# RMSNorm with SiLU on one core: six blocks of four rows in flight become four slots of six rows, with loads and stores on other queues

## The chip, the core and the metric

The kernel runs on one core of a Trainium2 chip. The core has a TensorE (PE), a VectorE (DVE), a ScalarE (ACT), a GpSimd (POOL) and a SyncE (SP); data come from the chip's memory (HBM) into the on-chip memory of 128 partitions by DMA. In this profile the core's transfers run on 16 DMA engines, and a transfer is issued from the queue of SP or of ACT. The metric is the device time of one execution in microseconds (us). The time before is the median of three runs.

## The reference

```python
def setup_inputs():
    batch, seq_len, hidden = 8, 1024, 2048
    return {
        "x": np.random.randn(batch, seq_len, hidden).astype(np.float32),
        "gamma": np.random.randn(hidden).astype(np.float32),
        "eps": np.float32(1e-5),
    }

def reference(x: np.ndarray, gamma: np.ndarray, eps: np.float32) -> np.ndarray:
    rms = np.sqrt(np.mean(x ** 2, axis=-1, keepdims=True) + eps)
    out = gamma * x / rms
    return (out * (1 / (1 + np.exp(-out)))).astype(np.float32)
```

There are 8192 rows of 2048 floats. Each row is divided by its root mean square, multiplied by gamma, and put through SiLU. 67.1 MB are read and 67.1 MB written.

## The kernel before

The rows are cut into 16 blocks of 512. A block lies on 128 partitions with four rows (J = 4) on each, one after the other, so that a partition holds 32 KB that are contiguous in HBM too. Six blocks (BUFS = 6) can be on the chip at once. In this text a "row" of a block means row j of all partitions: 128 x 2048 floats, 1 MB.

Before the blocks, gamma comes in as one row by a DMA from SP (L110), four matmuls with a column of ones spread it over the partitions (L113), and DVE copies it out of PSUM to g (L115). ACT then copies one element of the same tile (L116), which holds it until the copy to g is done; after that it issues loads 2 to 5. Loads 0 and 1 are issued before.

The work on one block:

- load (L54): one DMA of 4 MB from ACT's queue.
- squares: the sum of squares of each row, of which ACT takes the first one or two (L65, Square with accumulation) and DVE the others (L73). share(b) says how many ACT takes.
- root and invert: ACT's Sqrt of the mean plus eps (L82), DVE's reciprocal (L87).
- multiply: DVE multiplies each row by its reciprocal root and by g, in place (L92).
- silu: ACT's Silu on two rows at a time, in place (L98), then the store.
- store (L102): one DMA of 4 MB from SP's queue.

ACT needs a table load when it goes from Square or Silu to Sqrt, and from Sqrt to Silu; these are rows of their own in the profile.

The order is written out by hand (the body under manual_schedule is issued in the order of the program, engine by engine). In the loop over b, the squares and the root of block b + 1 are issued beside the multiply and silu of block b: for the first three blocks, ACT's squares of b + 1 come before the silus of b and DVE's squares of b + 1 after the multiplies of b; in the middle, all squares and the root of b + 1 come before the multiplies and silus of b. The load of block b + 3 is issued from ACT after its first square of block b + 1, once six blocks are under way; it waits for the store of the block that had its buffer. The last block is done differently: DVE multiplies by g alone (L155), the reciprocal comes between, and ACT's Silu takes it as its scale, row by row (L157); one store follows.

Of the kernel before, what the change touches and what calls it, by code (L numbers as in the profile page):

```python
# [1 line left out]

# [4 lines left out]

ACT = mybir.ActivationFunctionType
ALU = mybir.AluOpType


@with_exitstack
def kernel(
    ctx: ExitStack,
    tc: tile.TileContext,
    x: bass.AP,
    gamma: bass.AP,
    eps: bass.AP,
    out: bass.AP,
):  # L20

    nc = tc.nc
    P = nc.NUM_PARTITIONS
    f32 = mybir.dt.float32
    x2 = x.flatten_outer_dims()
    o2 = out.flatten_outer_dims()  # L30
    n, d = x2.shape
    J = 4
    BUFS = 6
    nblk = n // (P * J)
    xb = x2.rearrange("(b p j) d -> b p (j d)", p=P, j=J)
    ob = o2.rearrange("(b p j) d -> b p (j d)", p=P, j=J)

    singles = ctx.enter_context(tc.tile_pool(name="singles", bufs=1))
    pool = ctx.enter_context(tc.tile_pool(name="pool", bufs=BUFS))
    small = ctx.enter_context(tc.tile_pool(name="small", bufs=2))  # L40
    psum = ctx.enter_context(tc.tile_pool(name="psum", bufs=1, space=bass.MemoryType.PSUM))

    Q = 4
    w = d // Q
    g = singles.tile([P, d], f32)
    eps_t = singles.tile([P, 1], f32)
    ones = singles.tile([P, P], f32)
    junk_a = psum.tile([P, d], f32, name="junk_a")
    junk_v = psum.tile([P, d], f32, name="junk_v")
    blocks, sss, rmss, rstds = {}, {}, {}, {}  # L50

    def load(b):
        xt = pool.tile([P, J * d], f32, name="xt")
        nc.scalar.dma_start(out=xt, in_=xb[b])  # L54
        blocks[b] = xt

    def row(b, j):
        return blocks[b][:, j * d:(j + 1) * d]

    def squares_scalar(b, loads=()):  # L60


        sss[b] = small.tile([P, J], f32, name="ss")
        for j in range(share(b)):
            nc.scalar.activation(out=junk_a, in_=row(b, j), func=ACT.Square,  # L65
                                 accum_out=sss[b][:, j:j + 1])
            if j == 0:
                for s in loads:
                    load(s)

    def squares_vector(b):
        for j in range(share(b), J):
            nc.vector.tensor_tensor_reduce(  # L73
                out=junk_v, in0=row(b, j), in1=row(b, j), scale=1.0, scalar=0.0,
                op0=ALU.mult, op1=ALU.add, accum_out=sss[b][:, j:j + 1])

    def share(b):
        return 1 if 4 <= b <= 12 and b % 2 == 0 else 2

    def root(b):  # L80
        rms = small.tile([P, J], f32, name="rms")
        nc.scalar.activation(out=rms, in_=sss.pop(b), func=ACT.Sqrt, scale=1.0 / d, bias=eps_t)  # L82
        rmss[b] = rms

    def invert(b):
        rstd = small.tile([P, J], f32, name="rstd")
        nc.vector.reciprocal(out=rstd, in_=rmss.pop(b))  # L87
        rstds[b] = rstd

    def multiply(b):  # L90
        for j in range(J):
            nc.vector.scalar_tensor_tensor(out=row(b, j), in0=row(b, j), scalar=rstds[b][:, j:j + 1],  # L92
                                           in1=g, op0=ALU.mult, op1=ALU.mult)

    def silu(b):
        for h in range(0, J, 2):
            cols = slice(h * d, (h + 2) * d)
            nc.scalar.activation(out=blocks[b][:, cols], in_=blocks[b][:, cols], func=ACT.Silu)  # L98
        store(b)

    def store(b):
        nc.sync.dma_start(out=ob[b], in_=blocks[b])  # L102

    with tc.manual_schedule():

        load(0)
        nc.vector.memset(ones, 1.0)  # L107
        nc.vector.memset(eps_t, float(eps))
        nc.scalar.activation(out=junk_a[:, 0:1], in_=ones[:, 0:1], func=ACT.Square)  # L109
        nc.sync.dma_start(out=g[0:1, :], in_=bass.AP(tensor=gamma.tensor, offset=gamma.offset, ap=[[d, 1], [1, d]]))  # L110
        for c in range(Q):
            cols = slice(c * w, (c + 1) * w)
            nc.tensor.matmul(junk_v[:, cols], ones[0:1, :], g[0:1, cols], start=True, stop=True)  # L113
        load(1)
        nc.vector.tensor_copy(out=g, in_=junk_v)  # L115
        nc.scalar.copy(out=junk_a[:, 0:1], in_=junk_v[:, d - 1:d])  # L116
        for b in range(2, BUFS):
            load(b)

        last = nblk - 1
        SOON = 3
        squares_scalar(0)
        squares_vector(0)
        root(0)
        invert(0)
        for b in range(last):
            loads = [b + 3] if BUFS <= b + 3 < nblk else []
            if b < SOON:  # L130
                multiply(b)
                squares_scalar(b + 1, loads)
                silu(b)
                squares_vector(b + 1)
                root(b + 1)
            elif b < last - 1:
                squares_scalar(b + 1, loads)
                squares_vector(b + 1)
                root(b + 1)
                multiply(b)  # L140
                silu(b)
            else:
                multiply(b)
                squares_scalar(b + 1)
                silu(b)
                squares_vector(b + 1)
                root(b + 1)
            if b + 1 < last:
                invert(b + 1)


        for j in range(J):
            if j == J // 2:
                invert(last)
            nc.vector.tensor_mul(out=row(last, j), in0=row(last, j), in1=g)  # L155
        for j in range(J):
            nc.scalar.activation(out=row(last, j), in_=row(last, j), func=ACT.Silu,  # L157
                                 scale=rstds[last][:, j:j + 1])
        store(last)


# [1 line left out]
_INS = ['x', 'gamma', 'eps']  # L163
_OUTS = [((8, 1024, 2048), 'float32')]

_NUMBERS = {'eps': 9.999999747378752e-06}


# [26 lines left out]
```

## Time and profile before

| what | value |
|---|---|
| median of 3 runs | 317.02 us (316.7 to 317.08) |
| span of the profiled execution | 315.1 us |
| DVE busy | 235.3 us (75%), 157 instructions |
| ACT busy | 213.9 us (68%), 137 instructions |
| PE busy | 7.2 us (2%) |
| HBM read, written | 67.12 MB, 67.11 MB: 426 GB/s over the span |
| load: issue to landing, median | 38.7 us for 4 MB |
| store: issue to landing, median | 29.0 us for 4 MB |

The span runs from the first to the last instruction of one profiled execution; the runs' time has some 1.9 us more around it. An engine is busy while it executes an instruction; instructions that issue DMAs or wait are not counted. In the row of slices each digit is a tenth of busy time in one fortieth of the span (7.9 us). A group's row gives the line, the engine, the operation, its output and inputs, the count, then busy us and mean ns of one, then the idle time of the engine just before and what ended it. The chain of waits follows the work that ended last, backwards from the end. A DMA packet here is what one DMA engine moves for one partition of a transfer: 32 KB in a block's load or store. Each packet has a record with its start and its duration in the trace.

### The profile page before, as it was taken

The page shows a single profiled execution, that of the slowest core. Times are in us where ns is not written, and L with a number is a line of the kernel's source. Part 1 is how long each engine was busy: PE and PEld are TensorE (multiplying, and loading weights), DVE is VectorE, ACT ScalarE, POOL GpSimd, SP SyncE. Part 2 cuts the span into 40 slices and gives each one's busy share as a digit, 9 for nine tenths or more (in the row PEclk, how much of TensorE's full clock was granted, in tenths as well). Part 3 has the DMA queues.
Part 4 walks back from the last instruction along what each step waited for, and adds up shares of the span by engine and source line. Part 5 has one row for each costly group of instructions (what it writes and reads, how often), then busy time and mean ns, then how long its engine had stood idle before and what let it go on. Part 6 is the DMA issues. An engine that isn't in the chain of part 4 may idle for free.

```text
span 315.1 us, 439 instructions
## 1 busy us (share of the span) xinstructions
PE 7.2 (2%) x8; PEld 2.5 (1%) x8; DVE 235.3 (75%) x157; ACT 213.9 (68%) x137; POOL 0.2 (0%) x4
## 2 busy tenths in 40 slices
PE   6200000000000000000000000000000000000000
PEld 2000000000000000000000000000000000000000
DVE  0679697979895695957969489593995939999600
ACT  1269998972799258682687827877278768779910
POOL 0000000000000000000000000000000000000000
DMA  8999999999999999999999999999999999999997
GB/s 334 412 453 416 383 458 408 462 403 462 403 459 408 454 412 458 408 462 403 462 403 462 408 458 408 458 408 458 416 449 416 449 416 449 428 437 428 437 428 308
DMA packets 4613, 134.24 MB, mean 426 GB/s; under 512 B 514, under 2 KB 514, under 8 KB 514
## 3 DMA queue, kind: packets, MB, share of 16 engines
q10 hardware_dynamic: 2304, 67.11, 49.8%
q1 hardware_dynamic: 2306, 67.12, 49.3%
q14 instruction: 3, 0.02, 0.0%
HBM read 67.12 MB, written 67.11 MB: 426 GB/s over the span
## 4 chain that ended last, share of the span: by engine, by line
DMA 68%; DVE 14%; ACT 11%; issue 1%; ACTq 1%; DVEq 0%
DMA xt<-in_x_dram 68%; DVE xt L92 9%; DVE junk_v L73 5%; ACT xt L98 4%; ACT junk_a L65 3%; ACT xt L157 2%; ACT L82 1%; ACTq L190 1%; ACT L157 0%; ACT L98 0%; ACT rms L82 0%; DVE ss L73 0%; ACTq L54 0%; DVE rstd L87 0%; ACT L109 0%
## 5 line engine op out<-in xcount | busy, mean ns | idle before, releaser
L92 DVE SCALAR_TENSOR_TENSOR xt<-xt,rstd,g 128x2048 f32<-128x2048 f32 x60 | 137.0, 2346 | 0.1
L98 ACT ACTIVATE xt<-xt 128x4096 f32<-128x4096 f32 x30 | 108.3, 3615 | 27.4 <-DVE xt L92 27.4
L73 DVE CUSTOM_DVE_ANT_0 junk_v<-xt 128x2048 f32<-128x2048 f32 x37 | 85.1, 2299 | 42.9 <-DMA xt<-in_x_dram 42.2
L65 ACT ACTIVATE junk_a<-xt 128x2048 f32<-128x2048 f32 x27 | 50.7, 1876 | 16.1 <-DMA xt<-in_x_dram 14.0
L82 ACT ACT_TABLE_LOAD x15 | 19.2, 1283 | 26.6 <-DVE ss L73 26.5
L98 ACT ACT_TABLE_LOAD x14 | 18.0, 1283 | 0.2
L115 DVE COPY g<-junk_v 128x2048 f32<-128x2048 f32 x1 | 2.3, 2292 | 9.0 <-PE junk_v L113 9.0
L87 DVE RECIPROCAL rstd<-rms 128x4 f32<-128x4 f32 x16 | 2.7, 172 | 8.4 <-ACT rms L82 8.4
L155 DVE TENSOR_TENSOR xt<-xt,g 128x2048 f32<-128x2048 f32 x4 | 8.9, 2277 | 0.0
L82 ACT ACTIVATE rms<-ss,eps_t 128x4 f32<-128x4 f32 x16 | 4.8, 297 | 5.7 <-DVE ss L73 5.5
L157 ACT ACTIVATE xt<-xt,rstd 128x2048 f32<-128x2048 f32 x4 | 7.7, 1991 | 0.0
L113 PE MATMUL junk_v<-g,ones 1*128 1x512 f32 x8 | 7.2, 1072 | 2.8 <-DMA g<-in_gamma_dram 2.8
L116 ACT COPY junk_a<-junk_v 128x1 f32<-128x1 f32 x1 | 0.1, 144 | 9.8 <-DVE g L115 9.8
L73 DVE DVE_READ_ACCUMULATOR2_ANT ss<- 128x1 f32 x37 | 5.2, 141 | 0.0
L65 ACT ACTIVATION_READ_ACCUMULATOR junk_a<-xt 128x1 f32 x27 | 5.0, 186 | 0.0
L113 PEld LDWEIGHTS junk_v<-g,ones 1*128 1x128 f32 x8 | 2.5, 325 | 5.9 <-issue 5.9
L109 ACT ACT_TABLE_LOAD x1 | 1.3, 1283 | 1.1 <-PEq L176 1.1
L157 ACT ACT_TABLE_LOAD x1 | 1.3, 1283 | 0.0
L107 DVE MEMSET ones<- 128x128 f32 x1 | 0.2, 165 | 0.8 <-PEq L176 0.8
L109 ACT ACTIVATE junk_a<-ones 128x1 f32<-128x1 f32 x1 | 0.2, 174 | 0.0
L176 POOL MEMSET const-bfloat16-1.0<- 128x1 bf16 x1 | 0.1, 103 | 0.0
L176 POOL MEMSET const-uint8-127<- 128x1 uint8 x1 | 0.1, 102 | 0.0
(3 smaller groups left out, 0.3 us busy)
## 6 DMA issues: line engine op xcount, KB each, us to landing
xt<-in_x_dram ACTq DMA_DIRECT2D x16, 4096.0 KB, 38.7
out_dram<-xt SPq DMA_DIRECT2D x16, 4096.0 KB, 29.0
g<-in_gamma_dram SPq DMA_DIRECT2D x1, 8.0 KB
```

Source lines behind the costliest of these rows:

```text
L65: nc.scalar.activation(out=junk_a, in_=row(b, j), func=ACT.Square, accum_out=sss[b][:, j:j + 1])
L73: nc.vector.tensor_tensor_reduce(out=junk_v, in0=row(b, j), in1=row(b, j), scale=1.0, scalar=0.0, op0=ALU.mult, op1=ALU.add, accum_out=sss ...
L82: nc.scalar.activation(out=rms, in_=sss.pop(b), func=ACT.Sqrt, scale=1.0 / d, bias=eps_t)
L87: nc.vector.reciprocal(out=rstd, in_=rmss.pop(b))
L92: nc.vector.scalar_tensor_tensor(out=row(b, j), in0=row(b, j), scalar=rstds[b][:, j:j + 1], in1=g, op0=ALU.mult, op1=ALU.mult)
L98: nc.scalar.activation(out=blocks[b][:, cols], in_=blocks[b][:, cols], func=ACT.Silu)
L109: nc.scalar.activation(out=junk_a[:, 0:1], in_=ones[:, 0:1], func=ACT.Square)
L113: nc.tensor.matmul(junk_v[:, cols], ones[0:1, :], g[0:1, cols], start=True, stop=True)
L115: nc.vector.tensor_copy(out=g, in_=junk_v)
L155: nc.vector.tensor_mul(out=row(last, j), in0=row(last, j), in1=g)
L157: nc.scalar.activation(out=row(last, j), in_=row(last, j), func=ACT.Silu, scale=rstds[last][:, j:j + 1])
L190: with _tile.TileContext(nc) as tc:
```

## The change

The blocks have different sizes now: one of two rows, one of four, nine of six, and one of four, 64 rows of a partition as before. They live in four slots of six rows (48 KB of a partition); the first slot takes the blocks of two and four rows together at first. A block's DMA moves 16, 32 or 48 KB per partition, contiguous on both sides. Loads are issued from SP in the order of the blocks; the load into a slot that was used waits for all its stores. Stores are issued from ACT after the block's last Silu; the last block's store is two DMAs of two rows each. Gamma's load moves to ACT, and the copy of one element (L116 before) is gone.

compute(b) issues a whole block before the next one begins: half of the squares on DVE, half on ACT, Sqrt, reciprocal, multiplies, Silus, store. For blocks 0, 1, 2 and 11 (SCALED) DVE multiplies by g alone and the Silu takes the reciprocal root as its scale, row by row; the first of these multiplies is issued before the reciprocal. The others multiply by both on DVE and have Silus of two rows.

```diff
+FILLINGS = [
+    [(2, 2), (4, 4)],
+    [(6, 6)],
...
+    [(6, 6)],
+    [(4, 2)],
+]
+SLOTS = 4
+
+SCALED = (0, 1, 2, 11)
...
-    J = 4
-    BUFS = 6
...
-    pool = ctx.enter_context(tc.tile_pool(name="pool", bufs=BUFS))
-    small = ctx.enter_context(tc.tile_pool(name="small", bufs=2))
+    pool = ctx.enter_context(tc.tile_pool(name="pool", bufs=SLOTS))
+    small = ctx.enter_context(tc.tile_pool(name="small", bufs=3))
...
+    def load(b, slot):
+        b.slot = slot
+        nc.sync.dma_start(out=rows(b, 0, b.rows), in_=b.x)
...
+    def fill(k):
+        slot = pool.tile([P, ROWS * d], f32, name="xt")
+        for b in fillings[k]:
+            load(b, slot)
...
+    def compute(b):
+        J = b.rows
+        half = J // 2
...
+        for j in range(half):
             nc.vector.tensor_tensor_reduce(
+                out=junk_v, in0=rows(b, j), in1=rows(b, j), scale=1.0, scalar=0.0,
+                op0=ALU.mult, op1=ALU.add, accum_out=ss[:, j:j + 1])
+        for j in range(half, J):
+            nc.scalar.activation(out=junk_a, in_=rows(b, j), func=ACT.Square,
+                                 accum_out=ss[:, j:j + 1])
+        nc.scalar.activation(out=rms[:, 0:J], in_=ss[:, 0:J], func=ACT.Sqrt, scale=1.0 / d, bias=eps_t)
+        scaled = b.number in SCALED
         for j in range(J):
+            if j == (1 if scaled else 0):
+                nc.vector.reciprocal(out=rstd[:, 0:J], in_=rms[:, 0:J])
+            if scaled:
+                nc.vector.tensor_mul(out=rows(b, j), in0=rows(b, j), in1=g)
+            else:
+                nc.vector.scalar_tensor_tensor(out=rows(b, j), in0=rows(b, j), scalar=rstd[:, j:j + 1],
+                                               in1=g, op0=ALU.mult, op1=ALU.mult)
+        step = 1 if scaled else 2
+        for j in range(0, J, step):
+            if scaled:
+                nc.scalar.activation(out=rows(b, j), in_=rows(b, j), func=ACT.Silu,
+                                     scale=rstd[:, j:j + 1])
+            else:
+                nc.scalar.activation(out=rows(b, j, 2), in_=rows(b, j, 2), func=ACT.Silu)
+            k = b.per_store
+            if (j + step) % k == 0:
+                first = j + step - k
+                nc.scalar.dma_start(out=b.out[:, first * d:(first + k) * d], in_=rows(b, first, k))
 
     with tc.manual_schedule():
-
-        load(0)
+        slot = pool.tile([P, ROWS * d], f32, name="xt")
+        load(fillings[0][0], slot)
         nc.vector.memset(ones, 1.0)
         nc.vector.memset(eps_t, float(eps))
+        nc.scalar.dma_start(out=g[0:1, :], in_=bass.AP(tensor=gamma.tensor, offset=gamma.offset, ap=[[d, 1], [1, d]]))
         nc.scalar.activation(out=junk_a[:, 0:1], in_=ones[:, 0:1], func=ACT.Square)
-        nc.sync.dma_start(out=g[0:1, :], in_=bass.AP(tensor=gamma.tensor, offset=gamma.offset, ap=[[d, 1], [1, d]]))
...
-        load(1)
+        for b in fillings[0][1:]:
+            load(b, slot)
         nc.vector.tensor_copy(out=g, in_=junk_v)
-        nc.scalar.copy(out=junk_a[:, 0:1], in_=junk_v[:, d - 1:d])
-        for b in range(2, BUFS):
-            load(b)
...
+        for k in range(1, SLOTS):
+            fill(k)
+        for k in range(len(fillings)):
+            for b in fillings[k]:
+                compute(b)
+            if k + SLOTS < len(fillings):
+                fill(k + SLOTS)
```

More of the change, by code (lines that the diff above doesn't have):

```diff
@@ L9 @@
 ALU = mybir.AluOpType
+FILLINGS = [
+    [(2, 2), (4, 4)],
+    [(6, 6)],
+    [(6, 6)],
+    [(6, 6)],
+    [(6, 6)],
+    [(6, 6)],
+    [(6, 6)],
+    [(6, 6)],
+    [(6, 6)],
+    [(6, 6)],
+    [(4, 2)],
+]
+SLOTS = 4
+SCALED = (0, 1, 2, 11)
 @with_exitstack
@@ L31 @@
     n, d = x2.shape
-    J = 4
-    BUFS = 6
-    nblk = n // (P * J)
-    xb = x2.rearrange("(b p j) d -> b p (j d)", p=P, j=J)
-    ob = o2.rearrange("(b p j) d -> b p (j d)", p=P, j=J)
+    ROWS = max(sum(j for j, _ in f) for f in FILLINGS)
+    assert sum(j for f in FILLINGS for j, _ in f) * P == n
     singles = ctx.enter_context(tc.tile_pool(name="singles", bufs=1))
-    pool = ctx.enter_context(tc.tile_pool(name="pool", bufs=BUFS))
-    small = ctx.enter_context(tc.tile_pool(name="small", bufs=2))
+    pool = ctx.enter_context(tc.tile_pool(name="pool", bufs=SLOTS))
+    small = ctx.enter_context(tc.tile_pool(name="small", bufs=3))
     psum = ctx.enter_context(tc.tile_pool(name="psum", bufs=1, space=bass.MemoryType.PSUM))
@@ L49 @@
     junk_v = psum.tile([P, d], f32, name="junk_v")
[L50 to L90, printed above, removed]
-        for j in range(J):
[L92 to L99, printed above, removed]
@@ L101, in store @@
-    def store(b):
-        nc.sync.dma_start(out=ob[b], in_=blocks[b])
+    class Block:
+        pass
+    fillings, at, number = [], 0, 0
+    for f in FILLINGS:
+        blocks, r = [], 0
+        for j, per_store in f:
+            b = Block()
+            b.rows, b.per_store, b.offset, b.number = j, per_store, r, number
+            number += 1
+            b.x = x2[at:at + j * P, :].rearrange("(p j) d -> p (j d)", p=P, j=j)
+            b.out = o2[at:at + j * P, :].rearrange("(p j) d -> p (j d)", p=P, j=j)
+            blocks.append(b)
+            r += j
+            at += j * P
+        fillings.append(blocks)
@@ new lines, in load, with rows @@
+    def load(b, slot):
[5 more added lines that the diff above has]
+            load(b, slot)
+    def rows(b, j, k=1):
+        return b.slot[:, (b.offset + j) * d:(b.offset + j + k) * d]
+    def compute(b):
+        J = b.rows
+        half = J // 2
+        ss = small.tile([P, ROWS], f32, name="ss")
+        rms = small.tile([P, ROWS], f32, name="rms")
+        rstd = small.tile([P, ROWS], f32, name="rstd")
+        for j in range(half):
+            nc.vector.tensor_tensor_reduce(
+                out=junk_v, in0=rows(b, j), in1=rows(b, j), scale=1.0, scalar=0.0,
[5 more added lines that the diff above has]
+        scaled = b.number in SCALED
+        for j in range(J):
+            if j == (1 if scaled else 0):
[16 more added lines that the diff above has]
+                nc.scalar.dma_start(out=b.out[:, first * d:(first + k) * d], in_=rows(b, first, k))
@@ L113 @@
             nc.tensor.matmul(junk_v[:, cols], ones[0:1, :], g[0:1, cols], start=True, stop=True)
-        load(1)
+        for b in fillings[0][1:]:
+            load(b, slot)
         nc.vector.tensor_copy(out=g, in_=junk_v)
-        nc.scalar.copy(out=junk_a[:, 0:1], in_=junk_v[:, d - 1:d])
-        for b in range(2, BUFS):
-            load(b)
[L122 to L159, printed above, removed]
+        for k in range(1, SLOTS):
[5 more added lines that the diff above has]
+                fill(k + SLOTS)
 _INS = ['x', 'gamma', 'eps']
```

## The prediction

> **What bounds the kernel now.** I read the slices of the span first, then the stretches, then the chain, then the costliest groups. Slices and queues:
>
> ```profile
> DVE  0679697979895695957969489593995939999600
> ACT  1269998972799258682687827877278768779910
> DMA  8999999999999999999999999999999999999997
> DMA packets 4613, 134.24 MB, mean 426 GB/s; under 512 B 514, under 2 KB 514, under 8 KB 514
> q10 hardware_dynamic: 2304, 67.11, 49.8%
> q1 hardware_dynamic: 2306, 67.12, 49.3%
> ```
>
> The DMA row is 9 from the second slice to the last but one, while DVE and ACT have holes everywhere. q10 (loads) and q1 (stores) together took 99.1% of the 16 engines' time. The stretches (stretch, its length, five engines, clock, DMA share, GB/s):
>
> ```profile
> 24.00:34.00 10.00, 0.00 (x0) 0.00 (x0) 9.95 (x7) 9.94 (x7) 0.00 (x0) 1.00 1.01 436
> 34.00:42.00 8.00, 0.00 (x0) 0.00 (x0) 5.17 (x4) 7.91 (x8) 0.00 (x0) 1.00 0.97 373
> 42.00:66.00 24.00, 0.00 (x0) 0.00 (x0) 22.19 (x14) 21.23 (x11) 0.00 (x0) 1.00 1.01 437
> 66.00:279.00 213.00, 0.00 (x0) 0.00 (x0) 169.33 (x115) 144.74 (x90) 0.00 (x0) 1.00 1.00 433
> 279.00:300.00 21.00, 0.00 (x0) 0.00 (x0) 17.46 (x11) 20.68 (x13) 0.00 (x0) 1.00 1.00 434
> ```
>
> 433 GB/s is the pace with loads and stores mixed (66 to 279) and with stores nearly alone (from 279). Only 24 to 66 is below it: (10 x 436 + 8 x 373 + 24 x 437) / 42 = 424.6, so 42 x 8.4 / 433 = 0.8 us is lost where the first store comes in. The chain says the same, long stretches of loads end to end, and then the last block's work, under stores that still run:
>
> ```profile
> 104.80 38.98 DMA xt<-in_x_dram
> 143.78 0.02 issue
> 143.80 0.01 ACT junk_a L65
> 143.81 38.65 DMA xt<-in_x_dram
> ...
> 297.10 1.89 ACTq L190
> 298.99 1.89 ACT xt L157
> ```
>
> So the bytes bound it. 134.2 MB at 433 is 310.0 us. The span of 315.1 has 5.1 us more: about 2.1 until the first packet starts, 0.6 in the first packets (1.8 us each in the packet records instead of 1.21), 0.8 at the first store, 0.85 from the last packet to the end, and 0.8 that I don't resolve. The median of the runs, 317.02, is 1.9 above the span; I carry that over unchanged.
>
> **The change part by part.** "Row" is 8 KB on each of 128 partitions, 1.049 MB, or 2.42 us at 433 GB/s.
>
> *Longer runs.* A DMA gives each engine 8 packets, one per partition. Before: 32 block DMAs, 256 packets of 32 KB per engine. After: 12 loads and 13 stores, 200 packets of 16, 32 or 48 KB. Bytes are the same. What a packet costs beside its bytes comes from two records of different size in the packet records: 8 KB fetches in mid-run take 0.309 us, and the 32 KB packets 1.210 apiece by their count in 66 to 279 (175.9 per engine in 213 us). That makes 0.300 per 8 KB and 0.0085 fixed. Saved: 56 x 0.0085 = 0.48, and 7 semaphore packets of 0.009, 0.06. I take -0.5 us. Bounds: -0.1 if 48 KB packets pay in proportion to their bytes; -0.6 with 0.009, the whole time of a 4-byte packet, as the fixed part. The 48 KB size itself is in no row.
>
> [...]
>
> *Queues.* Loads go to SP, where 0.33 us (row of the gamma issue) replaces 0.38 (ACT's issue of block 0); both began at 0.73, so the first packet moves by under 0.1 us: nothing. L116, which held loads 2 to 5 back to 12.38, is gone; loads 0 and 1 covered that until 22.7, so nothing is gained. Thirteen stores cost ACT 13 x 0.4 = 5 us. Behind each on ACT wait the next block's squares; they wait for a load anyhow.
>
> *The first store.* It can start once g is there: copy of g ends at 12.3, DVE square 2.44, table load and sqrt 1.6, table load 1.28, two silus 3.9: issued near 21.5 instead of 35.18. Before, its first packet started 4.8 us after the issue, and two load packets per engine ran 0.4 us long each. I keep 0.8; bounds 0.4 (only half recurs) and 1.2 (it grows with 48 KB packets): -0.4 to +0.4.
>
> *Serial blocks.* No block's squares are now issued ahead of the block before's silus. These are the rows of the chain:
>
> ```profile
> L92 DVE SCALAR_TENSOR_TENSOR xt<-xt,rstd,g 128x2048 f32<-128x2048 f32 x60 | 137.0, 2346 | 0.1
> L98 ACT ACTIVATE xt<-xt 128x4096 f32<-128x4096 f32 x30 | 108.3, 3615 | 27.4 <-DVE xt L92 27.4
> L73 DVE CUSTOM_DVE_ANT_0 junk_v<-xt 128x2048 f32<-128x2048 f32 x37 | 85.1, 2299 | 42.9 <-DMA xt<-in_x_dram 42.2
> L82 ACT ACT_TABLE_LOAD x15 | 19.2, 1283 | 26.6 <-DVE ss L73 26.5
> ```
>
> From a landing to the store's issue, for six rows: three DVE squares 3 x (2.30 + 0.14) = 7.3 (ACT's three, 6.1, beside them), table load and sqrt 1.6, reciprocal 0.2, six multiplies at the pitch of 2.285 (four in 9.14) 13.7, the last pair's silu 3.6: 26.4 us. A block's bytes in and out need 12 x 2.42 = 29.1. So compute keeps up by 2.7 us a block. I cost it at nothing; the cover is the store queue. Followed from the start: store 0's first packet at about 27.5 (21.5, 4.8, and 1.2 for longer load packets), done by 47 (8 turns of a 16 KB store and a 48 KB load packet, 2.43 each); store 1 is ready at 37.6, done by 71 (8 turns of 3.03); store 2 is ready near 60, store 3 near 85, due at 100, then one in 29.1. Each is ready over 9 us before its turn. If the cover went, every us per block beyond it would be DMA idle time.
>
> *Four slots.* A refill on SP waits for all stores of its slot; only later loads queue behind it. Slot 0 is free at 71, and the loads already issued last to about 82: 11 us of cover, the same in later rounds. If it went, stores alone would keep the 433.
>
> *The tail.* Here it is closest. In the packet records of before, loads and stores take turns, one packet each apart from occasional pairs, and a packet takes 1.21 whether or not the other queue runs. So a load DMA pairs with a store DMA, whatever their sizes. By 27.5, (27.5 - 2.1 - 0.6 - 0.8) / 2.42 = 9.9 rows are loaded: blocks 0, 1 and 0.65 of block 2. The remaining 9.35 load DMAs pair with 9.35 stores, so when the last load ends, block 9 has 0.65 x 6 = 3.9 rows to store: 9.4 us. Block 10 landed 8 x (1.21 + 1.82) = 24.2 us earlier, and its first store packet is ready 26.4 + 0.4 issue + 1.3 (issue to first packet, from block 0) = 28.1 after landing, 3.9 after the last load. Slack 5.5 us. Block 11 follows on ACT: squares 4.1, table and sqrt 1.6, table 1.3, two silus 3.9, so its first half is ready some 12.6 us after block 10, whose store takes 14.5. The halves therefore hide behind it and gain nothing: the bytes already last to the end. I take 0.
>
> [...]
>
> Sum: 317.02 - 0.5 = 316.5, with bounds of -1.0 to +0.3 around 317.02.
>
> **The rivals.**
> 1. *Turns go by bytes, and the tail runs dry.* Then small stores don't lag, the store queue empties in the first blocks, and later each store starts when it is ready, 28.1 after its landing, 1.0 before block 10's landing. The last load needs 8 x 2 x 1.21 = 19.4 us beside it; in the 20.4 us block 9 has stored 4.2 rows, the other 1.8 take 4.4. The DMA is then idle from 23.8 to 28.1 after block 10's landing: 4.3 us less what is already prefetched; I take 3.3. It decides as soon as the 5.5 us of slack are gone, by this or by a slower chain. 316.5 + 3.3 = 319.8. For it: all sizes were equal before, so no row separates turns by packets from turns by bytes. Against it: packets run whole in the mixed stretch.
> 2. *The change doesn't do what it says: 48 KB runs are cut at 32 KB.* 18 six-row DMAs give 16 packets instead of 8: 344 per engine, 88 more than before x 0.0085 = +0.75, so 317.8. For it: no packet over 32 KB has been seen. Against it: 32 KB was whole.
> 3. *More is saved.* The first store's 0.8 goes too, since it is a small store that comes early: 316.5 - 0.8 = 315.7. Against it: the same two queues meet.
>
> **How the numbers follow.** About 0.2% (0.63 us) is what a measurement of this kernel can tell from no change: below 316.39 is faster, above 317.65 slower. Forecast, 0.62, at 316.5, own range 316.0 to 317.3: it straddles 316.39, so faster 0.28, same 0.34. Rival 1, 0.18: slower. Rival 2, 0.10: slower 0.07, same 0.03. Rival 3, 0.10: faster. Together faster 0.38, same 0.37, slower 0.25. The range goes from rival 3 to just over rival 1: 315.7 to 319.9.
>
> **What would show it.** DMA packets near 3,640 with the same bytes (2 x 1,600 data plus 400 semaphores and a few); over 5,900 is rival 2. A middle stretch at 433.5 to 434 GB/s. The first store issued near 21.5. DMA at 9 in all slices but the first and last: a hole near 285 to 290 is rival 1, a hole near 20 to 45 a dearer first store. Loads issued on SP as slots come free, 11 us before they are needed. What would make the prediction wrong above all is a DMA queue that is empty while blocks are being computed, or a pace that changes with the run's length.

## The result, and the profile after

| | before | after |
|---|---|---|
| median of 17 runs each | 316.96 us (316.7 to 317.31) | 317.78 us (317.06 to 321.07) |
| ratio to before, 95% interval | | 1.0041 (1.0029 to 1.0054) |
| span of the profiled execution | 315.1 us | 316.0 us |

The change makes the kernel slower: by 0.8 us on the median, where -0.5 was forecast, and by 0.4% or 1.3 us on the mean, from which the ratio is taken. The median hides the more telling part: before, all 17 runs lie within 0.6 us; after, within 4. In 29 runs of the changed kernel (these and the 12 of its repetition below) 18 lie between 317.06 and 318.03 (the lower group), five between 318.64 and 319.25, and six between 320.22 and 321.07.

The slices and queues of the changed kernel:

```profile
DVE  0797899879479657928891796579387927978700
ACT  1399999958784865767575857656674868579910
DMA  8999999999999999999999999999999999999986
DMA packets 3604, 134.24 MB, mean 425 GB/s; under 512 B 401, under 2 KB 401, under 8 KB 401
q1 hardware_dynamic: 1728, 67.11, 49.6%
q10 hardware_dynamic: 1874, 67.12, 49.1%
```

The DMA row is as full as before, but for the last two slices (8 and 6, where before had 9 and 7). 3604 packets are 3200 of the blocks, 401 of 4 bytes (16 for each of the 25 block DMAs and one for gamma), gamma's one and two instruction fetches: the 48 KB runs went whole (2304 packets of 49152 bytes). The 4-byte ones are called semaphore packets here, since the whole trace has as many semaphore updates by DMAs as packets of 4 bytes, 402. So rival 2 is not what happened, although its 317.8 is the measured median. Stretches of the same execution (stretch, length, engines, clock, DMA share, GB/s):

```profile
66.00:279.00 213.00, 0.00 (x0) 0.00 (x0) 157.35 (x97) 145.00 (x89) 0.00 (x0) 1.00 1.00 433
279.00:287.00 8.00, 0.00 (x0) 0.00 (x0) 6.37 (x5) 6.68 (x3) 0.00 (x0) 1.00 1.03 444
287.00:292.00 5.00, 0.00 (x0) 0.00 (x0) 3.75 (x5) 4.92 (x7) 0.00 (x0) 1.00 0.96 413
292.00:300.00 8.00, 0.00 (x0) 0.00 (x0) 6.53 (x3) 7.57 (x5) 0.00 (x0) 1.00 1.06 461
```

The middle still runs at 433, and the tail has no hole in this execution. A share a little over 1 or under it in so short a stretch is a matter of where its borders cut packets.

The costliest groups say that compute is what was costed: the same instructions at the same length, and more idle time in front of them.

```profile
L119 ACT ACTIVATE xt<-xt 128x4096 f32<-128x4096 f32 x24 | 86.8, 3617 | 43.4 <-DVE xt L111 43.4
L111 DVE SCALAR_TENSOR_TENSOR xt<-xt,rstd,g 128x2048 f32<-128x2048 f32 x48 | 109.3, 2347 | 0.3
L97 DVE CUSTOM_DVE_ANT_0 junk_v<-xt 128x2048 f32<-128x2048 f32 x32 | 73.6, 2300 | 47.4 <-DMA xt<-in_x_dram 46.7
```

The packet records of the trace give the account. They name no engine, but on one engine a packet starts 3 to 4 ns before the end of the one ahead of it, and so the records fall into 16 chains with equal data. From the start of one packet to the start of the next, one of 8, 16, 24, 32 or 48 KB takes 0.306, 0.607, 0.908, 1.209 or 1.812 us, which is 0.301 us per 8 KB plus 0.005 (24 KB from r1_cut24 below). "Ideal" is that, with 0.006 for a packet of 4 bytes; all numbers are means over the 16 engines:

| us | before | after | difference |
|---|---|---|---|
| ideal time of the packets | 309.8 | 309.5 | -0.32 |
| first packets, longer than ideal (first 5 us) | 0.54 | 0.87 | +0.33 |
| around the first store, longer than ideal (5 to 45 us) | 0.91 | 0.64 | -0.27 |
| later packets, longer than ideal | 0.08 | 0.29 | +0.21 |
| idle at the end, until the last engine is done | 0.52 | 1.39 | +0.87 |
| until an engine's first packet; 8 KB fetches | 0.46 | 0.34 | -0.12 |
| first to last packet | 312.3 | 313.0 | +0.7 |

The terms give the whole of the 0.7; another 0.15 of the longer span lies before the first packet and after the last. The large term is one the prediction has no place for: the 16 engines end their equal shares of 8.39 MB further apart. For each DMA the spread is the time between the first and the last of its 16 engines to end their data. Before, it is 0.5 to 0.6 us until 105 us and 0.84 from 117 to the end. After, it grows in steps, 0.75 at 70 us, 0.99 at 84, 1.43 at 172, 1.73 at 216, 1.89 at the end. Most steps are a single load packet that ran 0.2 to 0.5 us long on one engine.

### The profile page after: what moved, and what is told of

Read it like the earlier page. It is cut to its first block, busy times and chain, and to the rows that moved or that the text cites. A ratio compares the mean times of both kernels' runs of the same rounds, so it can differ in the third digit from the quotient of the medians.

```text
span 316.0 us, 411 instructions
## 1 busy us (share of the span) xinstructions
PE 7.2 (2%) x8; PEld 2.5 (1%) x8; DVE 224.3 (71%) x143; ACT 217.8 (69%) x142; POOL 0.2 (0%) x4
## 2 busy tenths in 40 slices
DMA packets 3604, 134.24 MB, mean 425 GB/s; under 512 B 401, under 2 KB 401, under 8 KB 401
## 4 chain that ended last, share of the span: by engine, by line
DMA 66%; DVE 20%; ACT 7%; issue 2%; SPq 0%; ACTq 0%
DMA xt<-in_x_dram 38%; DMA out_dram<-xt 28%; DVE xt L111 9%; DVE junk_v L97 7%; DVE xt L109 4%; ACT xt L116 3%; ACT xt L119 2%; ACT junk_a L101 1%; ACT L116 0%; ACT rms L103 0%; SPq L80 0%; ACTq L123 0%; DVE ss L97 0%; DVE rstd L107 0%; ACT L103 0%
## 5 line engine op out<-in xcount | busy, mean ns | idle before, releaser
L119 ACT ACTIVATE xt<-xt 128x4096 f32<-128x4096 f32 x24 | 86.8, 3617 | 43.4 <-DVE xt L111 43.4
L111 DVE SCALAR_TENSOR_TENSOR xt<-xt,rstd,g 128x2048 f32<-128x2048 f32 x48 | 109.3, 2347 | 0.3
L97 DVE CUSTOM_DVE_ANT_0 junk_v<-xt 128x2048 f32<-128x2048 f32 x32 | 73.6, 2300 | 47.4 <-DMA xt<-in_x_dram 46.7
L101 ACT ACTIVATE junk_a<-xt 128x2048 f32<-128x2048 f32 x32 | 60.2, 1882 | 25.0 <-DMA xt<-in_x_dram 22.7
L109 DVE TENSOR_TENSOR xt<-xt,g 128x2048 f32<-128x2048 f32 x16 | 35.8, 2280 | 0.0
L116 ACT ACTIVATE xt<-xt,rstd 128x2048 f32<-128x2048 f32 x16 | 31.0, 1993 | 0.8 <-ACT xt L116 0.4
L107 DVE RECIPROCAL rstd<-rms 128x6 f32<-128x6 f32 (+2 forms) x12 | 2.2, 186 | 16.5 <-ACT rms L103 16.5
L101 ACT ACTIVATION_READ_ACCUMULATOR junk_a<-xt 128x1 f32 x32 | 6.0, 186 | 0.0
L97 DVE DVE_READ_ACCUMULATOR2_ANT ss<- 128x1 f32 x32 | 4.5, 141 | 0.0
L103 ACT ACTIVATE rms<-ss,eps_t 128x6 f32<-128x6 f32 (+2 forms) x12 | 3.6, 299 | 0.1
```

The source lines that it names most:

```text
L97: nc.vector.tensor_tensor_reduce(out=junk_v, in0=rows(b, j), in1=rows(b, j), scale=1.0, scalar=0.0, op0=ALU.mult, op1=ALU.add, accum_out=s ...
L101: nc.scalar.activation(out=junk_a, in_=rows(b, j), func=ACT.Square, accum_out=ss[:, j:j + 1])
L103: nc.scalar.activation(out=rms[:, 0:J], in_=ss[:, 0:J], func=ACT.Sqrt, scale=1.0 / d, bias=eps_t)
L107: nc.vector.reciprocal(out=rstd[:, 0:J], in_=rms[:, 0:J])
L109: nc.vector.tensor_mul(out=rows(b, j), in0=rows(b, j), in1=g)
L111: nc.vector.scalar_tensor_tensor(out=rows(b, j), in0=rows(b, j), scalar=rstd[:, j:j + 1], in1=g, op0=ALU.mult, op1=ALU.mult)
```

## The experiments

All times are medians; ratios are of the means, to the kernel before on the same chip. A packet "ran long" where its record is more than 0.04 us longer than is usual for its size.

| run | what differs | us (lowest to highest, runs) | ratio, 95% interval |
|---|---|---|---|
| r1_after_again | nothing | 318.2 (317.23 to 320.69, 12) | 1.0055 (1.0029 to 1.008) |
| r1_cut24 | after, six rows as two DMAs | 318.25 (317.83 to 318.71, 5) | 1.0039 (1.0026 to 1.0052) |
| r1_four_rows | after, six slots of four rows | 319.62 (319.39 to 319.83, 4) | 1.0084 (1.0071 to 1.0097) |
| r1_before_swap | before, queues swapped | 317.22 (316.95 to 317.5, 11) | 1.0008 (0.9999 to 1.0016) |
| r2_tail_pieces | after, block 10's store in three | 317.73 (317.14 to 318.51, 8) | 1.0028 (1.0016 to 1.004) |
| r2_late_store | after, store 0 beside store 1 | 318.82 (317.87 to 319.3, 6) | 1.0051 (1.0038 to 1.0063) |
| r2_first_six | after, first block of six | 317.26 (316.99 to 317.45, 11) | 1.0012 (1.0003 to 1.002) |
| r3_before_shift04 | before, first store 0.4 us later | 316.98 (316.73 to 317.26, 11) | 1.0002 (0.9993 to 1.001) |
| r3_before_shift08 | before, first store 0.8 us later | 316.91 (316.65 to 317.89, 12) | 1.0003 (0.9993 to 1.0012) |
| r3_after_shift09 | after, first store 0.9 us later | 317.62 (317.15 to 318.59, 12) | 1.0025 (1.0016 to 1.0034) |
| r3_six_pieces | first_six and tail_pieces together | 317.92 (317.17 to 319.27, 12) | 1.0029 (1.0017 to 1.0042) |
| r4_tail_late | after, block 10's store 8.75 us later | 323.64 (323.11 to 325.86, 5) | 1.0234 (1.0207 to 1.0261) |

**The changed kernel once more** (r1_after_again, no edit).

> The changed kernel once more, as it stands, beside the three others on one chip. Every theory expects a ratio near 1.004. The point is the packet records of a second execution: in the first one the 16 DMA engines, which finish a transfer 0.84 us apart before the change, drifted to 1.89 us apart, in steps of about 0.3 us, each a single 48 KB load packet that ran long. If that is chance of one execution, the spread here is near 0.8 at the end and few load packets run long; if it belongs to the kernel, the spread is again above 1.5.

Its profile caught an execution of the upper group, with a span of 318.6. The tail in stretches:

```profile
279.00:287.00 8.00, 0.00 (x0) 0.00 (x0) 6.98 (x4) 6.18 (x3) 0.00 (x0) 1.00 0.99 428
287.00:292.00 5.00, 0.00 (x0) 0.00 (x0) 3.96 (x3) 4.59 (x3) 0.00 (x0) 1.00 0.71 305
292.00:300.00 8.00, 0.00 (x0) 0.00 (x0) 7.18 (x6) 7.91 (x8) 0.00 (x0) 1.00 1.12 485
```

From 287 to 292 the DMA share is 0.71: 5 x 0.29 = 1.5 us in which the engines had nothing (1.3 by the packet records). ACT's timeline says why. First the changed kernel's first profile, then this one (start us, us, instruction, and what its engine waited for): block 10's first square, and the issue of its store.

```profile
259.29 1.88 ACT L101 ACTIVATE junk_a<-xt 128x2048 f32<-128x2048 f32 x1 [2.44 <-DMA xt<-in_x_dram]
...
285.71 0.34 ACTq L123 DMA_DIRECT2D out_dram<-xt  x1
```

```profile
263.24 1.88 ACT L101 ACTIVATE junk_a<-xt 128x2048 f32<-128x2048 f32 x1 [2.58 <-DMA xt<-in_x_dram]
...
289.66 0.34 ACTq L123 DMA_DIRECT2D out_dram<-xt  x1
```

From landing to issue both take 26.4 us, the chain as it was priced. But block 10 landed 4 us later. The records show on which engines: on 14 of them 21 load packets went ahead of the first store packet, on two only 20. Those two stayed a turn behind with loads, and 13 of their load packets after 45 us ran long; all their packets from there on came to 2.7 and 2.9 us over the usual length, against 0.1 on most others. The spread of a load's completions rose from 2.2 us (block 2) to 5.6 (block 10). Block 10's compute began only after its slowest engine was done (in the first profile that engine's last packet ended at 257.10, the first square began at 259.29), so its store is late too, while the other 14 engines have run out of block 9's store. Two engines also ended some 2 us behind. The hole does not explain all of this execution: of the 2.6 us between the two profiles, 1.5 are the hole and the slower packets right behind it, 0.7 the later end of the slowest engine (2.07 against 1.39), and some 0.5 longer packets before.

**Shorter packets** (r1_cut24). The six-row loads and stores of after go as two DMAs each:

```diff
+        c = 3 if b.rows == 6 else b.rows
+        for j in range(0, b.rows, c):
+            nc.sync.dma_start(out=rows(b, j, c), in_=b.x[:, j * d:(j + c) * d])
...
```

> Same slots, same order of compute, same queues, but each six-row load and each six-row store goes as two DMAs of three rows, 24 KB per packet. Theory length (48 KB load packets run long now and then, so engines drift apart and the slowest sets the end): no long load packets in the middle, spread near 0.8 at the end, and since 24 KB packets cost 0.7 us more in fixed parts than 48 KB ones (18 more DMAs, 144 packets per engine less nothing, at 0.0085, and half of it off for the packets that were saved), a ratio of 1.001 to 1.003. Theory queue (loads on SP and stores on ACT make it): spread still above 1.5 and ratio 1.006. Theory first load (the 16 KB first packets cost 0.34 us more at the start, and the rest is chance): as queue, with the first 5 us unchanged at 0.88 us extra.

By the spacing of the packets, 144 of them at 0.005 and 18 semaphores at 0.006 are 0.8 us, near the 0.7 expected, though not by the way it was worked out. Measured is 318.25, a ratio of 1.0039, above the 1.003 of theory length. No run is above 318.71. Ten load packets after 45 us still ran long, one of them behind an instruction fetch, and the engines ended 1.63 us apart. So drift isn't the property of 48 KB alone.

**Four rows** (r1_four_rows):

```diff
...
+FILLINGS = [[(2, 2), (2, 2)]] + [[(4, 4)]] * 14 + [[(4, 2)]]
+SLOTS = 6
...
```

> The changed program with six slots of four rows: blocks of two and two, fourteen of four, and four rows, 32 KB packets as before the change, everything else of the new program kept (SP loads, ACT stores, a block computed whole before the next, last store in halves). Theory length: ratio 1.000 to 1.001, spread near 0.8. Theory queue: ratio above 1.004, spread above 1.5. Theory serial blocks (the new order of compute leaves the store queue empty): ratio above 1.004 with holes in the DMA row.

It is slower, 1.0084, with two gaps in the tail. This was not a clean test of the packets' length: with four rows the serial chain takes 2 x 2.44 + 1.6 + 0.2 + 4 x 2.285 + 3.6 = 19.4 us, as long as the block's bytes (8 x 2.42), so the store queue has no cover. The stretches show it (the same columns):

```profile
279.00:290.00 11.00, 0.00 (x0) 0.00 (x0) 9.11 (x5) 6.69 (x6) 0.00 (x0) 1.00 1.00 430
290.00:297.00 7.00, 0.00 (x0) 0.00 (x0) 6.97 (x6) 6.32 (x4) 0.00 (x0) 1.00 0.92 393
297.00:317.00 20.00, 0.00 (x0) 0.00 (x0) 6.77 (x5) 11.96 (x9) 0.00 (x0) 1.00 0.86 369
```

**Queues alone** (r1_before_swap): in the kernel before, loads on SP, stores and gamma on ACT.

> The kernel before with only the queues swapped: loads and no others on SP, stores and gamma on ACT. Theory queue: ratio 1.003 to 1.005, long load packets in the middle and the engines drift apart above 1.2 us. Theory length or first load: ratio 0.999 to 1.001, spread near 0.8.

1.0008, landings 0.98 us apart at the end; its two long load packets lie behind the 8 KB instruction fetches of those moments. The swap alone may cost something (the interval reaches 1.0016, 0.5 us), but not the 0.4%, and the drift doesn't come with it.

**Block 10's store in pieces** (r2_tail_pieces):

```diff
-    [(6, 6)],
+    [(6, 2)],
     [(4, 2)],
```

> The changed kernel with one edit: block 10 is stored in three DMAs of two rows, each issued after its own silu, so the first is ready some 9 us earlier than the store of six rows. Theory slack (the changed kernel's times fall into two groups, near 317.3 and near 320.5, because in the upper group block 10 lands 4 us late on its slowest engine and its store finds the store queue already empty): the upper group is gone, all runs between 316.9 and 318.3, median near 317.3, DMA share at 0.97 or more from 279 to 300. Theory skew (the 16 engines drift apart and the slowest sets the end, with or without the hole): runs above 319 are still there, ratio 1.004 or more.

None of the 8 runs is above 318.51. The profiled execution is as fast as before the change (315.2 us), although its load landings are 2.39 us apart:

```profile
279.00:287.00 8.00, 0.00 (x0) 0.00 (x0) 6.50 (x5) 6.68 (x3) 0.00 (x0) 1.00 0.96 416
287.00:292.00 5.00, 0.00 (x0) 0.00 (x0) 4.06 (x3) 4.95 (x5) 0.00 (x0) 1.00 0.92 397
292.00:300.00 8.00, 0.00 (x0) 0.00 (x0) 6.76 (x4) 7.54 (x7) 0.00 (x0) 1.00 1.00 426
```

Its shares of 0.96 and 0.92 miss the 0.97 that was expected, but the packet records have no idle engine between the first 5 us and the end, and the engines end 0.88 us apart. Only two load packets ran long after 45 us, both behind instruction fetches. The idle time at the end is 0.52 us, as in the kernel before, and with it the span is that of before. It is the shortest span among the profiled executions of the new program, and still 0.6 above the 314.6 that the forecast of 316.5 stands for. The ratio stays at 1.0028. That the pieces took the upper group away is not shown: the changed kernel itself was not run on this chip, and no run near 320 came in r1_cut24 and r3_after_shift09 either, which leave the tail's order as it was.

**The first store later** (r2_late_store): store 0 is issued just ahead of store 1.

> The changed kernel with the store of block 0 issued only after block 1's silus, just before block 1's own store, so the first store starts near 41 instead of 27 and loads keep the engines to themselves for 14 us longer. Nothing else moves. Theory slack: loads get 5 to 6 rows further ahead, block 10 lands 8 to 10 us before its store is due, the upper group of times is gone, median 317.0 to 317.5. Theory skew: the group near 320.5 stays, ratio 1.004 or more. If the turns of a 16 KB store packet and a 48 KB load packet are what makes engines differ, the spread of load landings stays above 2 us here too.

Loads did get ahead, and no run is near 320.5, but it is slower than expected: 318.82. In its profile (317.4) there is no idle engine in the tail, and the engines end 3.33 us apart; 35 load packets ran long after 45 us. This is drift by itself, without the hole: 2.6 us of mean idle time at the end against 0.5 before.

**A first block of six** (r2_first_six): the first filling is [(6, 6)].

> The first slot takes one block of six rows instead of blocks of two and four; eleven blocks, ten of six and one of four. The first packets are 48 KB and the first store starts near 45. Theory slack: as with the late store, no runs above 318.3; median 316.6 to 317.2, since 16 fewer packets per engine save 0.14 and the first load's extra goes back to that of before (0.54 instead of 0.88). Theory skew: runs above 319 stay. If unequal packets make the engines differ, the landings' spread is below 1.2 us here.

The narrowest and best of the new program, 1.0012. At 317.26 it lies just above the 316.6 to 317.2 that was expected: the first store cost 1.08 us in long packets where the kernel before has 0.91, the first packets 0.70 instead of 0.54. The landings' spread is 2.05, not under 1.2, so it was not unequal packets that set the engines apart here.

**The phase of the first store** (r3): one Square of some columns into the scratch tile ahead of block 0's last silu.

> The kernel before with one ACT instruction of about 0.4 us (a Square of 272 columns into the scratch tile) ahead of the last silu of block 0, so that the first store of the kernel comes 0.4 us later; nothing else is changed. Theory phase (the loads run back to back on 16 engines that stand 0.5 to 1 us apart; where the first store's packets reach them just at a packet boundary, some engines take the store one load packet sooner than others, stay one turn apart to the end, and run long load packets): either all engines again have the same number of load packets ahead of their first store packet, and the ratio is 0.999 to 1.001, or they are split and it is 1.002 or more. Of this run and the one with 0.8 us, a packet being 1.21 us, at least one should be split. Theory blocks (the loss comes with the blocks and their serial order, not with the phase): both at 1.000 and nothing split.

> The same with about 0.8 us (752 columns). Theory phase: see the run with 0.4 us; at least one of the two split, its landings spread over 1.5 us or more and its ratio 1.002 or more. Theory blocks: 1.000.

> The changed kernel with one ACT instruction of about 0.9 us (872 columns), half of a 48 KB packet, ahead of the last silu of block 0, so that its first store comes 0.9 us later. Theory phase: the two groups of times become one, either near 317.2 (all engines in step, no runs above 318.3) or near 320.5 (always split). Theory blocks: the two groups stay, 317.2 and 320.5, as in the changed kernel.

In the kernel before, both shifts did split the engines: ten took 31 load packets before the first store packet and six 30, and 14 against two in the other; landings were up to 2.18 us apart. And both cost nothing, 1.0002 and 1.0003, with not one load packet long after 45 us. So engines out of turn did no harm by themselves in these two runs, and the theory as it stood falls. In the changed kernel with the shift, none of 12 runs is above 318.59. But its profile doesn't have all engines in step: 13 took 21 load packets before the first store packet and three 22, and still only four load packets ran long and the span is 315.6. So why the upper group is missing there stays open.

**Both edits** (r3_six_pieces):

> One block of six rows in the first slot and block 9, the last of six rows, stored in three DMAs of two rows: the two edits that helped alone. If what is left after them is the engines' drift and the longer first packets, the median is 317.0 to 317.3 and the ratio 1.000 to 1.0015; if the tail's order was still at fault in the run with the first block of six, it is 316.4 to 316.8.

317.92, and up to 319.27: worse than the first block of six alone. 31 of its load packets after 45 us ran long. The two gains don't add.

**Block 10's store later** (r4_tail_late): five Squares ahead of its last silu.

```diff
+                for _ in range(5 if b.number == 10 and j == 4 else 0):
+                    nc.scalar.activation(out=junk_a, in_=g, func=ACT.Square)
```

> The changed kernel with five Squares of 2048 columns into the scratch tile ahead of block 10's last silu: some 9.2 us of ACT work, of which 0.9 fill a wait, so block 10's store is issued 8.3 us later and nothing before it moves. Theory slack: in the first profile of the changed kernel this store's first packet could have come 3.6 us before the engines ran out of block 9's, so the lower group moves from 317.3 to 317.3 + 8.3 - 3.6 = 322.0, the upper one, which has no slack left, from 320.5 to 328 or 329; a hole of about 4.7 us after 290 in the DMA row. If the tail isn't what sets the time (the drift of the engines alone does), the groups stay near 317.3 and 320.5.

The issue of the store, and the DMA row of the slices:

```profile
294.46 0.34 ACTq L125 DMA_DIRECT2D out_dram<-xt  x1
...
DMA  8999899999999999999999999999999999992997
```

The 2 near the end of the slices is the hole; in stretches:

```profile
287.00:292.00 5.00, 0.00 (x0) 0.00 (x0) 4.17 (x3) 4.94 (x4) 0.00 (x0) 1.00 0.14 59
292.00:297.00 5.00, 0.00 (x0) 0.00 (x0) 0.00 (x0) 4.55 (x4) 0.00 (x0) 1.00 0.37 157
```

The store was issued at 294.46 instead of 285.71, 8.75 us later. On the mean of the engines, block 9's store ended at 289.0 and block 10's began at 295.36: a hole of 6.4 us. So 2.4 us of the delay were cover, not the 3.6 of the expectation. The span is 321.1 instead of 316.0, only 5.1 longer, because the engines end 0.17 us apart after this hole and 1.89 in the first profile. The expected 322.0 is missed too: the lowest run is 323.11. No run reached the 328 expected for the upper group; the highest is 325.86.

## Why the prediction was wrong, step by step

*Longer runs: right in kind, too large in size.* The saving measured is 0.32 us, where 0.5 was taken and 0.1 to 0.6 allowed. The records last 0.309 and 1.213 us for 8 and 32 KB, but they overlap the next packet by 3 to 4 ns. The forecast set the length of the one (0.309) against the spacing of the other (1.210) and so got 0.0085 fixed; from start to start it is 0.005.

*Queues: right, as far as shown.* 1.0008 for the swap alone, at most 1.0016; on the mean of the engines, loads start at 2.03 against 2.07.

*The first store: right.* Issued at 21.77 (forecast 21.5), first packet at 26.6 (27.5); long packets cost 0.64 there, 0.27 less than before, within the bounds. That the first packets, now 16 KB, would cost 0.33 more was not thought of.

*Serial blocks and slots: right.* 26.4 us from landing to issue, with the table load of 1.28 us that was counted ahead of each Sqrt (12 of 12; before it was 15 of 16, and the Sqrt at 75.58 had none: since the one at 67.90 ACT had done only a Square); stores 0 and 1 done at 45.6 and 69.7 (47 and 71); a block every 29.0; the DMA is fed in all of the middle.

*The end: this step failed, and it decides the usual run.* "the bytes already last to the end. I take 0" treats 16 engines as one. The time from the mean engine's end to the last one's is a term of its own. It was 0.5 us in the 0.8 that "I don't resolve", and was carried over unchanged. It is 0.4 to 0.7 in the four profiles of the old program, swapped and shifted too; in the new one 1.39 in the first profile, 2.07 in the second, and 0.5 (the pieces) to 2.6 (the late store) in the variants without a hole. It eats the saving even where no hole opens. The profile's 316.0 is 1.4 above the 314.6 of the forecast: 0.87 for the end, 0.33 for the first packets, 0.21 for later long packets, 0.18 for the smaller saving, less 0.27 at the first store, and small rests.

*The tail: its slack was mis-sized.* "Slack 5.5 us" is 2.5 in the first profile. The count by turns was right: 21 load packets ahead of the first store, which is block 2 at 0.63 (forecast 0.65); on each engine 24.2 us from block 10's last packet to the last load (24.2), and 9.06 more of block 9's store (9.4). Turns went by packets (four exceptions in some 1900 from 60 to 250 us), so rival 1's mechanism didn't come. The 1.0 us that it takes off its hole as already prefetched is shown by no run; with the engines idle, block 10's first packet came 0.9 us after its issue (r4_tail_late). But block 10's store can start 30.8 us after the mean engine's last packet of that block, not 28.1. The chain of 26.4 begins 3.4 us later than was counted: 1.25 until the slowest engine has its last packet (257.10), and 2.2 from there to the first square (259.29), since the semaphore packet takes a turn of its own, behind one more store packet of 1.8 us, and the report comes some 0.35 us after it. From issue to first packet it is then 0.9 and not 1.7. In the second profile the slowest engine is another 4 us late, which is more than the slack. The hole opens where rival 1 put it, for another reason: late landing, not early stores. The forecast said that the tail decides "as soon as the 5.5 us of slack are gone"; the delayed store shows that it does, once some 2.4 us are gone.

*Open.* Why load packets run long in the new program: 18 and 24 of 1074 after 45 us in its two profiles, 2 to 35 in its other variants with 48 KB packets, none of 1536 in the kernel before, shifted or not. Two in each profile with 48 KB packets, and both of those in the swapped kernel, lie behind an instruction fetch; the others do not. Not the queues alone, not the turns alone, not 48 KB alone. Length, addresses and the serial order were not separated from each other, since the one run meant for that ran into its compute chain. Open too is whether all of the slower runs have a hole: one of them was profiled, and the changed kernel was not run again on the chips of the later rounds. Some of these numbers are from single executions that differ by much (2 long packets in one, 35 in another), so they rank nothing.

None of the runs beats the kernel before.

## What to carry to other kernels

This DMA-bound kernel ended with the slowest of its 16 engines, 0.5 us after their mean before and 1.39 after, and each block landed with its slowest. Slack that is counted for "the DMA" had to cover the spread of the engines, here 0.8 to 5.6 us, and the turn in which the completion is reported, here 1.2 or 1.8 us; where it didn't, a hole opened (1.3 us in r1_after_again). This kernel was at 433 GB/s from 66 to 279 us already, and fewer and longer packets saved only their fixed part, 0.005 us each, 0.32 in all with the semaphore packets; in such a case look first at what the new order takes from the slack at the tail. When a cost per packet is worked out, take all packets in the same way, from start to start. Read the lowest and highest of many runs too, since their spread was the first sign.

## What the runs showed of the hardware

- From start to start a packet takes 0.301 us per 8 KB plus 0.005, from 8 to 48 KB (before and after; 24 KB from r1_cut24); its record is 3 to 4 ns longer and overlaps the next.
- While both queues had work, load and store packets alternated one by one on each engine, 32 KB with 32 KB before, 48 KB with 32 or 48 KB after (60 to 250 us, two and four exceptions in some 2800 and 1900 packets). The 4-byte semaphore packet took a turn too: a load's came one store packet (1.21 us before, 1.81 after) behind its last data.
- While loads streamed, the first packet of the first store started 4.4 to 5.5 us after its issue (means of the engines, 14 profiles; 4.65 before, 4.80 after). With the engines idle it was 0.8 to 1.0 us (r1_after_again, r4_tail_late), and for the first load of the kernel 1.2 to 1.4 (1.29 before, 1.28 after).
- After the hole of 6.4 us the engines ended 0.17 us apart (r4_tail_late); in the profiles without a hole, 0.8 (before) to 3.3 (r2_late_store).
- An 8 KB instruction fetch sat on one engine alone, 0.31 us, and the packet behind it was 0.1 to 0.5 us longer in 28 of 30 cases (before 0.12 and 0.36, after 0.53 and 0.25).
